# Taking turns between a small and a large expert in a two-layer diffusion backbone

## The chip, the core and the metric

The kernel runs on one core of a Trainium2 chip. The time is the device time of one execution in microseconds (us); the number for a kernel is the median of its runs. The engines are named as the profile names them: PE (TensorE, matrix products), DVE (VectorE), ACT (ScalarE), POOL (GpSimd), SP (SyncE, which issues the weight loads).

## What is computed

The kernel computes a backbone of two layers over 256 latent tokens and 256 context tokens of width 1024. Layer 0 is a gated short convolution and a dense SwiGLU, layer 1 is differential attention and a mixture of experts. The change is in the mixture of experts alone. Cut to that, the reference is:

```python
logits = (a @ w_r) + b_r                       # 256 tokens, 8 experts
top_v, top_i = lax.top_k(logits, 2)            # each token goes to 2 of 8
gates = jax.nn.softmax(top_v, axis=-1)
# every expert e, for the tokens that chose it:
#   y_e = (silu(x_e @ w1[e]) * (x_e @ w3[e])) @ w2[e]     1024 -> 2816 -> 1024
# out[token] = sum over its experts of gate * y_e[token]
h = h + g2 * out
```

All weights are float32, and the result has to be as good as float32. PE's fast form takes operands rounded to a shorter mantissa (fp32r). So most weights are split into a rounded part and the remainder, and both are multiplied.

## The kernel before

**Experts.** Experts 0 and 1 are handled first. The other six are sorted on the chip by how many tokens chose them, and the places 2, 4 and 6 get the three with the fewest tokens (`FEW`, line 37). A place in `FEW` has room for 64 tokens (a "small" expert below), every other place for 128 (a "large" one). Two neighbouring places make a pair: (0,1), (2,3), (4,5), (6,7). The tokens of a pair are gathered together (`gather`, line 1177: eight steps, each of four matmuls into a tile `g` and a few small DVE and ACT operations). `returns` (line 1213) makes the matrices that bring a pair's results back to their tokens.

**Chunks and units.** An expert's weights come in 33 units of 1 MB, three to a chunk, so there are 11 chunks to an expert and 88 in all (`chunks`, line 162: expert by expert). A chunk multiplies two units into a hidden tile (`up`, line 1243; tile `h13`, called h in the profile) and one unit from hidden to output (`down`, line 1282; the accumulators `y`). Between them are the activation (`act`, line 1251) and a turn to the other layout (`hidden`, line 1261). In a large expert a unit costs PE 12 matmuls of 512 columns: the activations too are split in two, and three of the four products are made. In a small expert the two halves of the tokens share one operand, and a unit costs 8.

**The split.** Every unit goes DMA to a raw tile, then ACT rounds it (line 88, tile `wh`), then DVE subtracts (line 92, tile `wl`), each in two halves of 128x1024. There are three pairs of tiles (wh, wl). `Parts.unit` (line 98) hands out the next unit, gives back the pair of the unit before, and at once emits ACT's and DVE's work for the unit two further on. Engines execute in program order, so this work stands in the queues of ACT and DVE between the activation work of the chunks.

**Unsplit units.** In a small expert the second unit of every odd chunk (five of 11) is `whole` (lines 171 to 178): it is multiplied as plain float32 from the raw tile, with four matmuls in place of eight. That takes nothing from ACT or DVE and needs no pair of tiles.

**`hidden` of a small chunk** (lines 1263 to 1273) is a zigzag: PE adds the halves with `fold` (tile `ht`), ACT applies silu (`hg`, line 1267), DVE multiplies (`hg`, line 1268), ACT rounds (`hh`, line 1271), DVE subtracts (`hh`, line 1272). For a large chunk PE transposes, ACT rounds (`hh`, line 1278), DVE subtracts (`hl`, line 1279). DVE also makes the product `ga` (line 1258) in `act`.

**The order of a chunk's work** (loop at line 1345): first unit, `down` of the chunk two before, `hidden` of the chunk before, second unit, `act`. When an expert has ended, `weighted` (line 1296) splits its result (ACT `yh`, DVE `yl`), and `spread` (line 1305) adds it to the tokens in four pieces: each four matmuls into a tile `g`, then two DVE operations on `xl` (line 1315). Gather steps stand at the end of the chunks 3 to 10 of a large expert.

**PSUM** has eight banks: two for `g`, two for `y`, two for h, two for `ht` (lines 1321 to 1324).

Of the kernel before, what the change touches and what calls it, by code (L numbers as in the profile page):

```python
# [11 lines left out]
F32 = mybir.dt.float32  # L12
# [4 lines left out]
OP = mybir.AluOpType  # L17
AX = mybir.AxisListType
PSUM = bass.MemoryType.PSUM

P = 128
D = 1024
KT = D // P
# [12 lines left out]

FEW = (2, 4, 6)
H = P // 2
LAM = 0.8 - 0.6 * math.exp(-0.3)
# [103 lines left out]
def backbone(ctx: ExitStack, tc: tile.TileContext, i, out):  # L143
# [35 lines left out]
    uses += [(NE - 1, 3 * c + 2) for c in (NCH - 2, NCH - 1)]  # L179
    units += [moe_unit(*u) for u in uses]  # L180
# [996 lines left out]
    def gather(pr=None):  # L1177
# [4 lines left out]
        if pr is not None and 2 * pr in FEW:  # L1182
            both = xs[0][0]
            xs[0] = [both[:, :, :H], both[:, :, H:], both]
            cols[0] = slice(H, P)
# [118 lines left out]

    def spread(n, w, back):

        for k in range(4 * n, 4 * n + 4, 2):
            ps = psg.tile([P, 2, T], F32, name="g")
            for j in range(2):
                c = slice((k + j) % 4 * P, ((k + j) % 4 + 1) * P)  # L1310
                for b in range(2):
                    PE.matmul(ps[:, j], w[b][:, c], back, start=b == 0, stop=b == 1)
            for j in range(2):
                x = X[0][k + j]
                V.scalar_tensor_tensor(x, ps[:, j], mod1[20 + k // 2][:, j, 0:1], x, op0=OP.mult, op1=OP.add)  # L1315
# [10 lines left out]
    def acc():  # L1326
        return [psy.tile([P, T2], F32, name=f"y{n}") for n in range(2)]

# [4 lines left out]
    parts.holding = True  # L1333
    res, parted, acts, hids, y = None, deque(), {}, {}, None

    def finish(g):

        result = y
        e, c = chunks[g]
        if c == 0:  # L1340
            result = acc()
        down(result, hids.pop(g), parts.unit(), c == 0, c == NCH - 1)
        return result

    for g, (e, c) in enumerate(chunks):
        n, pr, few_now = e % 2, e // 2, e in FEW
        ps = psh.tile([P, T2], F32, name="h13")
# [6 lines left out]
        if g == 0:  # L1354
            next(run)
            for _ in range(2):
                parts.give(1)
            parts.holding = False
        if g > 1:
            y = finish(g - 2)  # L1360
            if chunks[g - 2][1] == NCH - 1:
                e0 = chunks[g - 2][0]
                res = y, rets[e0 // 2][1][:, e0 % 2:e0 % 2 + 1], rets[e0 // 2][0][:, e0 % 2]
        if g > 0:
            hids[g - 1] = hidden(acts.pop(g - 1), chunks[g - 1][0] in FEW)
        if res is not None:
            parted.extend((m, v, res[2]) for m, v in enumerate(weighted(*res[:2])))
            res = None
        elif parted:
            spread(*parted.popleft())  # L1370
        if g == 1:
# [7 lines left out]
        for k in range(0, 4, 2):  # L1379
            up(ps, got[pr][n], 1, w, [k, k + 1])  # L1380
        acts[g] = act(ps, few_now)
        if parted and c > 1:
            spread(*parted.popleft())
        if n == 0 and c == 4:
            rets[pr] = returns(pr)
        if n == 1 and e < NE - 1:
            if c == 1:
                for t in range(2):
                    onehot(t, pr + 1)
                run = gather(pr + 1)  # L1390
            if 3 <= c < 3 + KT:
                got[pr + 1] = next(run)
    y = finish(g - 1)
    hids[g] = hidden(acts.pop(g))
    y = finish(g)
    for n, w in enumerate(weighted(y, rets[3][1][:, 1:2])):
        spread(n, w, rets[3][0][:, 1])
        write(n)

# [3 lines left out]
    with tc.If(count[0] > 0):  # L1403
        for e in range(NE):
            with tc.If(count[1 + e] > 0):
# [6 lines left out]
                back, gs = returns(e // 2)  # L1412
                y = acc()
                for c in range(NCH):
# [12 lines left out]
                for m, w in enumerate(weighted(y, gs[:, n:n + 1])):  # L1427
                    spread(m, w, back[:, n])
        for n in range(2):
# [82 lines left out]
```

## Time and profile before

| | |
|---|---|
| median of 3 runs | 1592.47 us (1592.3 to 1595.17) |
| the profiled execution's own time | 1594.94 us |
| its span, first to last instruction | 1592.3 us |
| PE busy over the span | 1540.4 us (97%) |
| DVE busy | 1278.5 us (80%) |
| ACT busy | 864.8 us (54%) |
| DMA | 400.35 MB, mean 251 GB/s |
| mixture of experts | from about 820 us to the end |
| mean granted TensorE clock | 0.985 |

In the profile, busy time is the time in which an engine executes. Matmuls overlap in a pipeline, so the time of one matmul in a row is longer than the step from one to the next; the steps are read from the start times. A line of the timeline gives start, length, engine, line of the source, operation, output and inputs, and how many like operations are merged in it. In square brackets stands the time in which the engine was idle just before, and who ended that.

### The profile page before, as it was taken

What the parts mean: (1) busy time and instruction counts of PE and PEld (TensorE: products, weight loads), DVE (VectorE), ACT (ScalarE), POOL (GpSimd) and SP (SyncE); (2) the same over time, 40 slices, a digit from 0 to 9 for tenths busy, and PEclk for the clock granted to TensorE, in tenths of its full rate; (3) what the DMA queues carried; (4) which work ended last, traced back from release to release, by engine and by line L of the source; (5) the groups of instructions that cost most, each with busy time, mean ns of one, the idle gap of its engine ahead of it and who ended that gap; (6) DMA issues with size and microseconds to landing.
All of it is one profiled execution on the core that took longest, in us unless ns stands there. A gap on an engine that the chain in (4) does not pass through costs nothing. (4 is left out here: it accounts for less than half of the span.)

```text
span 1592.3 us, 20866 instructions
## 1 busy us (share of the span) xinstructions
PE 1540.4 (97%) x7569; PEld 1259.1 (79%) x7569; DVE 1278.5 (80%) x1880; ACT 864.8 (54%) x1244; POOL 44.7 (3%) x162
## 2 busy tenths in 40 slices
PE   8899899999999999999889999999999999999997
PEld 7687689888888888888777888877787777877785
DVE  5888887758838848666669899988999889998996
ACT  3232235222212334444557777877788786777774
POOL 0000000000000001211200000000000000000000
PEclk9899999999999999999989999999999999999999
DMA  9345543535527621422338999999999999999990
GB/s 369 111 159 185 191 159 112 184 128 196 204 103 281 251 102 54 159 80 80 133 134 340 362 353 342 342 394 407 364 353 361 388 421 346 347 369 402 395 366 29
DMA packets 55729, 400.35 MB, mean 251 GB/s; under 512 B 6449, under 2 KB 6481, under 8 KB 7105
## 3 DMA queue, kind: packets, MB, share of 16 engines
q1 hardware_dynamic: 55298, 398.50, 66.1%
q8 instruction: 61, 1.00, 0.3%
q0 software_dynamic: 320, 0.44, 0.2%
q14 instruction: 50, 0.41, 0.1%
HBM read 397.87 MB, written 1.05 MB: 251 GB/s over the span
## 5 line engine op out<-in xcount | busy, mean ns | idle before, releaser
L92 DVE TENSOR_TENSOR wl<-rw,wh 128x1024 fp32r<-128x1024 f32 (+1 forms) x208 | 315.9, 1548 | 86.4 <-ACT wh L88 85.8
L88 ACT CAST wh<-rw 128x1024 fp32r<-128x1024 f32 (+1 forms) x207 | 263.3, 1309 | 61.1 <-PE mm L200 56.4
L199 PE MATMUL mm<-ah,wh 128*128 128x512 f32 (+1 forms) x576 | 222.0, 385 | 5.6 <-ACT ah L339 4.7
L201 PE MATMUL mm<-ah,wl 128*128 128x512 f32 (+1 forms) x576 | 221.4, 384 | 5.1 <-DVE wl L92 5.0
L200 PE MATMUL mm<-al,wh 128*128 128x512 f32 (+1 forms) x576 | 221.1, 384 | 0.0
L92 DVE TENSOR_TENSOR wl<-rp,wh 128x1024 fp32r<-128x1024 f32 (+1 forms) x152 | 183.3, 1246 | 17.9 <-ACT wh L88 17.2
L279 DVE SCALAR_TENSOR_TENSOR junk<-ra,cb 128x1024 bf16<-128x1024 f32 x136 | 166.3, 1222 | 3.3
L88 ACT CAST wh<-rp 128x1024 fp32r<-128x1024 f32 (+1 forms) x152 | 155.4, 1070 | 2.6 <-PE h L1240 2.4
L1239 PE MATMUL h<-wh,xs 128*128 128x512 f32 x352 | 142.4, 404 | 0.0
L1241 PE MATMUL h<-wl,xs 128*128 128x512 f32 x352 | 138.9, 395 | 0.0
L1240 PE MATMUL h<-wh,xs 128*128 128x512 f32 x352 | 138.8, 394 | 0.0
L199 PEld LDWEIGHTS mm<-ah,wh 128*128 128x128 f32 x576 | 110.8, 192 | 27.9 <-ACT ah L339 6.0
L201 PEld LDWEIGHTS mm<-ah,wl 128*128 128x128 f32 x576 | 110.3, 192 | 27.7 <-DVE wl L92 7.1
L200 PEld LDWEIGHTS mm<-al,wh 128*128 128x128 f32 x576 | 110.5, 192 | 21.5 <-DVE al L334 0.9
L92 DVE TENSOR_TENSOR wl<-rq,wh 128x1024 fp32r<-128x1024 f32 x102 | 119.5, 1219 | 9.9 <-ACT wh L88 9.4
L92 DVE TENSOR_TENSOR wl<-ra,wh 128x1024 fp32r<-128x1024 f32 x96 | 113.0, 1218 | 6.7 <-ACT wh L88 6.1
L88 ACT CAST wh<-rq 128x1024 fp32r<-128x1024 f32 x102 | 101.2, 1048 | 2.1 <-PE h L1240 2.1
L88 ACT CAST wh<-ra 128x1024 fp32r<-128x1024 f32 x96 | 95.9, 1048 | 0.0
L1241 PE MATMUL y<-wl,hh 128*128 128x512 f32 x220 | 87.4, 397 | 0.6 <-DVE wl L92 0.5
L1239 PE MATMUL y<-wh,hh 128*128 128x512 f32 x220 | 87.1, 396 | 0.5 <-ACT hh L1278 0.5
L1240 PE MATMUL y<-wh,hl 128*128 128x512 f32 x220 | 86.9, 395 | 0.0
L199 PE MATMUL mm<-wh,ah 128*128 128x256 f32 (+1 forms) x256 | 83.7, 327 | 0.0
(330 smaller groups left out, 2988.7 us busy)
## 6 DMA issues: line engine op xcount, KB each, us to landing
rw<-moe SPq DMA_DIRECT2D x81, 1024.0 KB, 7.1
rp<-moe SPq DMA_DIRECT2D x79, 1024.0 KB, 7.1
rw<-w SPq DMA_DIRECT2D x61, 1024.0 KB, 4.8
ra<-moe SPq DMA_DIRECT2D x52, 1024.0 KB, 7.1
rq<-moe SPq DMA_DIRECT2D x52, 1024.0 KB, 7.0
ra<-ada SPq DMA_DIRECT2D x44, 1024.0 KB, 4.9
rx<-ada SPq DMA_DIRECT2D x4, 1024.0 KB, 19.9
rp<-w SPq DMA_DIRECT2D x4, 1024.0 KB, 6.3
```

The costliest lines, as they stand in the source:

```text
L88: self.nc.scalar.copy(hi[:, c0], raw[:, c0])
L92: engine.tensor_tensor(out=lo[:, c], in0=raw[:, c], in1=hi[:, c].bitcast(F32), op=OP.subtract)
L199: PE.matmul(ps, wh, xh, start=first, stop=False)
L200: PE.matmul(ps, wh, xl, start=False, stop=False)
L201: PE.matmul(ps, wl, xh, start=False, stop=last)
L279: V.scalar_tensor_tensor(junk, raw[:, a * D:(a + 1) * D], 1.0, cb[:, s], op0=OP.mult, op1=OP.mult, accum_out=m[:, a, s:s + 1])
L1239: PE.matmul(ps, xh, wh, start=first, stop=False)
L1240: PE.matmul(ps, xl, wh, start=False, stop=False)
L1241: PE.matmul(ps, xh, wl, start=False, stop=last)
```

## The change

Chunks of experts 0 and 1 stay as they are, one expert after the other. From place 2 on, the chunks of the two experts of a pair take turns: small chunk 0, large chunk 0, small chunk 1, and so on. The load order (`uses`) follows from it. Only the chunks 3 and 7 of a small expert have an unsplit unit, so two in place of five, and nine units in all are newly split. Two experts are open at once, so `y` takes four banks; `g` and `ht` fall from two banks to one each. `spread` now does one piece at a time, and a list (`todo`, taken from by `point` three times in a chunk) sets where the pieces and the second result of a pair stand. `returns` stands at chunk 6, and the gather of the next pair runs along both experts' chunks 7 to 10 of the present pair. At the end the last small expert's four pieces stand after the last `down`, ahead of the last large expert's. The small experts' gathered activations get two buffers.

```diff
+WHOLE = (3, 7)
-    chosen, chunks = [], [(e, c) for e in range(NE) for c in range(NCH)]
+    chosen, chunks = [], [(e, c) for e in range(2) for c in range(NCH)]
+    chunks += [(2 * pr + n, c) for pr in range(1, NE // 2) for c in range(NCH) for n in range(2)]
...
-        if e in FEW and c % 2:
+        if e in FEW and c in WHOLE:
             whole.append(len(units) + len(uses))
...
-    psg = fin.enter_context(tc.tile_pool(name="psg", bufs=2, space=PSUM, reuse_waits="tile"))
+    psg = fin.enter_context(tc.tile_pool(name="psg", bufs=1, space=PSUM, reuse_waits="tile"))
...
-    pst = fin.enter_context(tc.tile_pool(name="pst", bufs=2, space=PSUM, reuse_waits="tile"))
+    pst = fin.enter_context(tc.tile_pool(name="pst", bufs=1, space=PSUM, reuse_waits="tile"))
+    def acc(e):
+        return [psy.tile([P, T2], F32, name=f"y{e % 2}{n}") for n in range(2)]
...
+        if g > 1 and chunks[g - 2][1] == NCH - 1:
+            e0 = chunks[g - 2][0]
+            if e0 < 2:
+                result(e0)
+                todo.extend([None, piece, None, piece, piece, None, piece])
...
+                result(e0)
+                todo.extend([None, piece, None, piece, piece, other, None, None, piece, piece, piece, None, piece])
...
-        if n == 0 and c == 4:
+        if n == 0 and c == 6:
             rets[pr] = returns(pr)
...
+        if pr < NE // 2 - 1 and (n == 1 and c >= 1 if pr == 0 else 2 * c + n >= 13):
...
+    finish(g - 1)
     hids[g] = hidden(acts.pop(g))
+    result(NE - 2)
+    finish(g)
+    for m in range(2):
+        for k in range(2):
+            spread(*parted.popleft())
+    result(NE - 1)
+    for m in range(2):
+        for k in range(2):
+            spread(*parted.popleft())
+        write(m)
```

How this moves the order on DVE is seen in the middle of a pair. Before, in the small expert of the pair (4,5) by itself, two chunks hold five splits (`wl`, each row the two halves of a unit), and each chunk the two steps of the zigzag (`hg`, `hh`):

```order
L1272 TENSOR_TENSOR hh<-hg,hh 128x2x64
L92 TENSOR_TENSOR wl_77<-rw_71,wh_76 128x1024 x2
L92 TENSOR_TENSOR wl_79<-rw_73,wh_78 128x1024 x2
L92 TENSOR_TENSOR wl_75<-ra_69,wh_74 128x1024 x2
L1268 TENSOR_TENSOR hg<-ht,hg 128x128
L1272 TENSOR_TENSOR hh<-hg,hh 128x2x64
L92 TENSOR_TENSOR wl_77<-rp_4397,wh_76 128x1024 x2
L92 TENSOR_TENSOR wl_79<-rw_72,wh_78 128x1024 x2
L1268 TENSOR_TENSOR hg<-ht,hg 128x128
L1272 TENSOR_TENSOR hh<-hg,hh 128x2x64
```

Now, in the middle of a pair, on the same engine (`ga` and `hl` belong to the large chunk):

```order
L1272 TENSOR_TENSOR hg<-ht,hg 128x128
L1276 TENSOR_TENSOR hh<-hg,hh 128x2x64
L94 TENSOR_TENSOR wl_77<-rw_71,wh_76 128x1024 x2
L1262 TENSOR_TENSOR ga<-h_11440,ga 128x256
L94 TENSOR_TENSOR wl_79<-rp_4396,wh_78 128x1024 x2
L94 TENSOR_TENSOR wl_75<-rq_6528,wh_74 128x1024 x2
L1283 TENSOR_TENSOR hl<-ht,hh 128x256
L94 TENSOR_TENSOR wl_77<-ra_70,wh_76 128x1024 x2
L94 TENSOR_TENSOR wl_79<-rw_72,wh_78 128x1024 x2
L94 TENSOR_TENSOR wl_75<-rp_4397,wh_74 128x1024 x2
L1272 TENSOR_TENSOR hg<-ht,hg 128x128
L1276 TENSOR_TENSOR hh<-hg,hh 128x2x64
```

A zigzag is now followed by six splits and the two steps of a large chunk before the next zigzag comes; the zigzag itself, and the split that stands right behind it, are as they were.

At the end of the program DVE before had the last expert's `yl` and four pieces (`xl`, two operations each):

```order
L1258 TENSOR_TENSOR ga<-h_12204,ga 128x256
L1279 TENSOR_TENSOR hl<-ht,hh 128x256
L1302 SCALAR_TENSOR_TENSOR yl_12296<-y_11703,gs,yh_12294 128x512
L1302 SCALAR_TENSOR_TENSOR yl_12297<-y_11704,gs,yh_12295 128x512
L1315 SCALAR_TENSOR_TENSOR xl<-g,mod_20_3728,xl 128x256 x2
L1315 SCALAR_TENSOR_TENSOR xl<-g,mod_21_3771,xl 128x256 x2
L1315 SCALAR_TENSOR_TENSOR xl<-g,mod_22_3802,xl 128x256 x2
L1315 SCALAR_TENSOR_TENSOR xl<-g,mod_23_3844,xl 128x256 x2
```

Now the same place has the results of two experts, one behind the other, each piece through the one bank of `g`:

```order
L1262 TENSOR_TENSOR ga<-h_12240,ga 128x256
L1283 TENSOR_TENSOR hl<-ht,hh 128x256
L1306 SCALAR_TENSOR_TENSOR yl_12320<-y_11132,gs,yh_12318 128x512
L1306 SCALAR_TENSOR_TENSOR yl_12321<-y_11133,gs,yh_12319 128x512
L1318 SCALAR_TENSOR_TENSOR xl<-g,mod_20_3728,xl 128x256 x2
L1318 SCALAR_TENSOR_TENSOR xl<-g,mod_21_3771,xl 128x256 x2
L1318 SCALAR_TENSOR_TENSOR xl<-g,mod_22_3802,xl 128x256 x2
L1318 SCALAR_TENSOR_TENSOR xl<-g,mod_23_3844,xl 128x256 x2
L1306 SCALAR_TENSOR_TENSOR yl_12368<-y_11202,gs,yh_12366 128x512
L1306 SCALAR_TENSOR_TENSOR yl_12369<-y_11203,gs,yh_12367 128x512
L1318 SCALAR_TENSOR_TENSOR xl<-g,mod_20_3728,xl 128x256 x2
L1318 SCALAR_TENSOR_TENSOR xl<-g,mod_21_3771,xl 128x256 x2
```

Four pieces and one `yl` pair of the last small expert, which stood among the last large expert's chunks, now stand behind all chunks.

## Rows read from the trace of the kernel before

**Rows 1.** Busy time by stage: length, each engine's busy time, clock, DMA share, GB/s.

```profile
1021.86:1107.77 85.91, 85.86 (x394) 65.13 (x393) 75.85 (x94) 66.70 (x94) 0.00 (x0) 1.00 0.99 390
1107.77:1207.22 99.45, 98.04 (x456) 79.63 (x455) 92.23 (x119) 76.99 (x109) 0.00 (x0) 1.00 0.94 360
1021.86:1207.22 185.36, 183.90 (x848) 144.76 (x847) 168.08 (x212) 143.68 (x202) 0.00 (x0) 1.00 0.96 374
1392.58:1573.64 181.06, 180.37 (x819) 141.50 (x818) 164.87 (x193) 138.78 (x185) 0.00 (x0) 1.00 0.85 338
```

**Rows 2.** DVE timeline in small expert 2: two chunks, five splits.

```profile
1069.54 0.28 DVE L1268 TENSOR_TENSOR hg<-ht,hg 128x128 f32<-128x128 f32 x1
1070.18 0.29 DVE L1272 TENSOR_TENSOR hh<-hg,hh 128x128 fp32r<-128x128 f32 x1 [0.36 <-ACT hh L1271]
1071.13 4.74 DVE L92 TENSOR_TENSOR wl<-ra,wh 128x1024 fp32r<-128x1024 f32 x4 [0.65 <-ACT wh L88]
1075.79 0.28 DVE L1268 TENSOR_TENSOR hg<-ht,hg 128x128 f32<-128x128 f32 x1
...
1077.40 2.36 DVE L92 TENSOR_TENSOR wl<-rw,wh 128x1024 fp32r<-128x1024 f32 x2 [0.67 <-ACT wh L88]
...
1084.31 0.28 DVE L1268 TENSOR_TENSOR hg<-ht,hg 128x128 f32<-128x128 f32 x1
```

**Rows 3.** ACT timeline in the same chunk.

```profile
1084.63 0.30 ACT L1271 CAST hh<-hg 128x128 fp32r<-128x128 f32 x1 [1.88 <-DVE hg L1268]
```

**Rows 4.** PE timeline in the same expert: an unsplit unit's chunk, then a split one.

```profile
1081.60 3.65 PE L1235 MATMUL h<-rp,xl 128*128 128x512 f32 x8
...
1089.63 0.71 PE L1235 MATMUL h<-wh,xl 128*128 128x512 f32 x2
...
1096.15 1.08 PE L1235 MATMUL h<-ra,xl 128*128 128x512 f32 x2
```

**Rows 5.** DVE timeline in large expert 3.

```profile
1122.96 1.40 DVE L1302 SCALAR_TENSOR_TENSOR yl<-y,gs,yh 128x512 fp32r<-128x512 f32 x2
1124.28 2.35 DVE L92 TENSOR_TENSOR wl<-ra,wh 128x1024 fp32r<-128x1024 f32 x2
1126.55 0.42 DVE L1258 TENSOR_TENSOR ga<-h,ga 128x256 f32<-128x256 f32 x1
...
1132.54 1.65 DVE L1315 SCALAR_TENSOR_TENSOR xl<-g,mod,xl 128x256 f32<-128x256 f32 x4
```

**Rows 6.** DVE timeline in expert 3: the splits behind two gather steps.

```profile
1147.75 2.36 DVE L92 TENSOR_TENSOR wl<-rw,wh 128x1024 fp32r<-128x1024 f32 x2 [1.46 <-ACT wh L88]
...
1173.39 2.36 DVE L92 TENSOR_TENSOR wl<-rp,wh 128x1024 fp32r<-128x1024 f32 x2 [0.45 <-ACT wh L88]
```

**Rows 7.** PE timeline in large expert 7: the transposes of two neighbouring chunks.

```profile
1561.85 0.38 PE L1275 MATMUL ht<-ident,ga 128*128 128x128 f32 x2
...
1570.43 0.38 PE L1275 MATMUL ht<-ident,ga 128*128 128x128 f32 x2
```

**Rows 8.** ACT timeline: the copy between the two `g` tiles of `returns`.

```profile
1063.42 0.59 ACT L1220 CAST back<-g 128x512 fp32r<-128x512 f32 x1
```

**Rows 9.** The first gather on PE and DVE; last the busy time of the stage behind.

```profile
820.85 0.41 PE L1196 MATMUL g<-oh,nh 128*128 128x256 f32 x1
821.34 0.53 DVE L1203 TENSOR_SCALAR gx<-g,mod 128x256 f32<-128x256 f32 x1
821.92 0.58 PE L1196 MATMUL g<-oh,nh 128*128 128x256 f32 x1
830.00:842.00 12.00, 10.21 (x39) 7.56 (x38) 8.94 (x15) 9.25 (x13) 0.00 (x0) 0.86 0.48 184
```

**Rows 10.** The end of the program on PE and DVE.

```profile
1579.97 0.40 PE L1241 MATMUL y<-wl,hh 128*128 128x512 f32 x1
1581.89 3.42 DVE L1315 SCALAR_TENSOR_TENSOR xl<-g,mod,xl 128x256 f32<-128x256 f32 x8
1582.91 0.36 PE L1312 MATMUL g<-back,yh 128*128 128x256 f32 x1 [0.59 <-DVE xl L1315]
```

More of the change, by code (lines that the diff above doesn't have):

```diff
@@ L1182, in gather @@
         if pr is not None and 2 * pr in FEW:
-            both = xs[0][0]
+            both = xs[0][pr % 2]
             xs[0] = [both[:, :, :H], both[:, :, H:], both]
@@ L1303, in weighted, with spread @@
         return list(zip(yh, yl))
[L1305 to L1315, printed above, removed]
+    def spread(k, w, back):
+        ps = psg.tile([P, 2, T], F32, name="g")
+        for j in range(2):
+            c = slice((k + j) % 4 * P, ((k + j) % 4 + 1) * P)
+            for b in range(2):
+                PE.matmul(ps[:, j], w[b][:, c], back, start=b == 0, stop=b == 1)
+        for j in range(2):
+            x = X[0][k + j]
+            V.scalar_tensor_tensor(x, ps[:, j], mod1[20 + k // 2][:, j, 0:1], x, op0=OP.mult, op1=OP.add)
     def write(n):
@@ L1333, in backbone, with result, piece, point @@
     parts.holding = True
-    res, parted, acts, hids, y = None, deque(), {}, {}, None
+    parted, acts, hids, ys = deque(), {}, {}, {}
     def finish(g):
-        result = y
         e, c = chunks[g]
         if c == 0:
-            result = acc()
-        down(result, hids.pop(g), parts.unit(), c == 0, c == NCH - 1)
-        return result
+            ys[e] = acc(e)
+        down(ys[e], hids.pop(g), parts.unit(), c == 0, c == NCH - 1)
+    def result(e):
+        back, gs = rets[e // 2]
+        n = e % 2
+        for m, v in enumerate(weighted(ys.pop(e), gs[:, n:n + 1])):
+            parted.extend((4 * m + k, v, back[:, n]) for k in (0, 2))
+    def piece():
+        spread(*parted.popleft())
+    todo = deque()
+    def point():
+        f = todo.popleft() if todo else None
+        if f is not None:
+            f()
     for g, (e, c) in enumerate(chunks):
-        n, pr, few_now = e % 2, e // 2, e in FEW
+        n, pr = e % 2, e // 2
         ps = psh.tile([P, T2], F32, name="h13")
@@ L1358, in backbone, with other @@
             parts.holding = False
+        point()
         if g > 1:
[L1360 to L1363, printed above, removed]
+            finish(g - 2)
         if g > 0:
             hids[g - 1] = hidden(acts.pop(g - 1), chunks[g - 1][0] in FEW)
[L1366 to L1370, printed above, removed]
+        point()
+        if g > 1 and chunks[g - 2][1] == NCH - 1:
[3 more added lines that the diff above has]
+                todo.extend([None, piece, None, piece, piece, None, piece])
+            elif e0 in FEW:
+                def other(e0=e0):
+                    piece()
+                    result(e0 + 1)
+                result(e0)
+                todo.extend([None, piece, None, piece, piece, other, None, None, piece, piece, piece, None, piece])
         if g == 1:
@@ L1380, in backbone @@
             up(ps, got[pr][n], 1, w, [k, k + 1])
-        acts[g] = act(ps, few_now)
-        if parted and c > 1:
-            spread(*parted.popleft())
-        if n == 0 and c == 4:
+        acts[g] = act(ps, e in FEW)
+        point()
+        if n == 0 and c == 6:
             rets[pr] = returns(pr)
-        if n == 1 and e < NE - 1:
-            if c == 1:
+        if pr < NE // 2 - 1 and (n == 1 and c >= 1 if pr == 0 else 2 * c + n >= 13):
+            if pr + 1 not in got:
+                got[pr + 1] = None
                 for t in range(2):
@@ L1412, in backbone @@
                 back, gs = returns(e // 2)
-                y = acc()
+                y = acc(0)
                 for c in range(NCH):
```

17 lines of the change are left out of this document (6 added, 11 removed).

## The prediction

> **What bounds the kernel now.** I read the busy time by stage first, over the third to the last pair of experts, since the change touches little before them. One pair takes 185.36 us, the last one, which gathers for nobody, 181.06 us up to its last chunk's activation [rows 1]. PE is busy for 183.90 of the 185.36 us at the full granted clock, ACT for 143.68, and DVE for 168.08, which is 91% [rows 1]. So PE looks like the bound and DVE like an engine with 17.3 us to spare. The DMA share is 0.96 at 374 GB/s, and it reached 390 GB/s in the small expert's stage [rows 1].
>
> The second look is at DVE's spare time, in its timeline. In a small expert, two chunks with five splits take 1084.31 - 1069.54 = 14.77 us [rows 2]. Three splits take 1084.31 - 1077.40 = 6.91 us, so one takes 2.30. The zigzag takes from 1069.54 to 1071.13, and again from 1075.79 to 1077.40: 1.6 us, of which only 0.57 is work. In the rest DVE waits 0.36 us for ACT's hh and 0.65 us for ACT's next wh. ACT in its turn had waited 1.88 us for DVE's hg [rows 3]. The two engines stand in each other's way: ACT cannot round the next unit before hh, since hh is ahead of it in its queue, and hh needs hg, which DVE reaches late. So DVE's chain is 5 x 2.30 + 2 x 1.6 = 14.7 us, which is all of the 14.77. PE needs for the same two chunks 1096.15 - 1081.60 = 14.55 us [rows 4]. In this stage DVE is a little slower than PE, with 88% busy (75.85 of 85.91).
>
> In a large expert a chunk costs PE 1570.43 - 1561.85 = 8.58 us [rows 7], and DVE three splits with ga and hl at 0.42 each [rows 5], 7.7 us. With gather steps DVE waits again, 1.46 us behind an even step and 0.45 behind an odd one [rows 6]. Adding up a pair for DVE: 61 splits x 2.30 = 140.3; eleven zigzags and eleven times ga and hl, 11 x 2.44 = 26.8; two results, each 1.32 for yl (1124.28 - 1122.96) and four pieces at 0.8 (1.65 for two) [rows 5], 9.0. That is 176.1 us. What is left of 185.4 is 9.3 us, and eight gather steps with 4 x (1.46 + 0.45) = 7.6 us of waits and their own work fill it. So the 17.3 us are not spare: 11 x 1.02 = 11.2 us lie in the zigzags and most of the rest behind the gather steps. **PE and DVE's chain are both full over a pair.**
>
> **The change part by part.** First the turn-taking with three more splits to a pair. In a plain pair of chunks (small split, large) PE needs 6.52 (1096.15 - 1089.63, a split chunk's work [rows 4]) + 8.58 = 15.1 us. DVE's chain needs 6 x 2.30 + 1.6 + 0.84 = 16.2 us. Taking turns does not shorten the zigzag: its two waits come from the order on ACT and DVE, which the new order keeps. So a plain pair runs at DVE's 16.2, and PE begins to wait. Per pair of experts DVE gets 3 x 2.30 = 6.9 us more, and PE is freed of 3 x 1.51 us (8.03 for the chunk with the unsplit unit, 1089.63 - 1081.60, less 6.52 [rows 4]), which is worth nothing while DVE is late. **Three pairs: 20.7 us.** Bounds: below, PE sets the pace (the first rival); above, add the pairs with an unsplit unit. There PE needs 16.6 and DVE 13.9 us, and DVE can use the 2.7 us only as far ahead as the three tile pairs let it. That is two units of PE, 1.9 + 2.8 us (8.58/3 and 8 of a large unit's 12 matmuls), less the half rounding and half subtraction (some 1.0 and 1.2) that must be over: 2.4 us. I take 1 us in all for what is lost there; nothing absorbed would be 6 x 2.7 = 16 us.
>
> The last small expert's yl and pieces leave the pairs: 1.32 + 4 x 0.8 = **-4.5 us** on DVE there.
>
> One bank for g in `returns`: the second tile now waits until ACT has copied the first. The copy is 0.59 us [rows 8], and it stands behind the activation in ACT's queue; PE's small matmuls and DVE's copy of gs follow it. Bounds are 0 and about twice the copy; I take 0.6 each, four times: **2.4 us**.
>
> One bank for g in the first gather, before any chunk: five steps run on PE one after the other. Before, the third waited for the first step's evacuation: it starts at 821.92, and DVE's gx had run from 821.34 to 821.87 [rows 9]. Now each step waits for its own evacuation. The second would start at 821.92 in place of 820.85, and a step then costs its matmuls (0.9, a little under the 1.07 us from the second step's start to the third's, which hold a short wait), 0.53 us of evacuation and two handovers, some 1.55 in place of about 1.0. Five steps make 2.8 us; two more gathers behind the first matmuls have the same pause. The splits of the first chunk stand behind the gather's casts on ACT, so they come later too. **3.5 us**, bounds 2 and 6.
>
> Pieces of expert 0 stand right ahead of two gather steps of expert 1, and share the one bank: PE must wait for DVE's two xl, which stand behind a split and ga. At most 1.3 us twice; DVE's chain is close to PE's there, which hides some. **1.5 us**, bounds 0 and 3.
>
> The end: before, PE's last down ends at about 1580.2, and DVE's last xl at 1581.89 + 3.42 = 1585.31 [rows 10], 5.1 us. Two banks let eight xl run without a pause, and PE's third piece waits 0.59 us. With one bank a piece is PE's four matmuls with their latency (0.63), DVE's two xl (0.86) and two handovers, 1.65 us. Eight pieces and yl between them make some 13.9 us. Against that, the last down but one is a small expert's, 0.9 us shorter, and DVE has no split left at that point. **7 us**, bounds 5 and 9.
>
> DMA: a pair now asks for the same 66 units in more time, at steadier demand, so it stays hidden. The loads wait for tiles on SP; nothing is moved past it. Experts 0 and 1 keep their chunks.
>
> **How the sum stands.** 20.7 + 1 - 4.5 + 2.4 + 3.5 + 1.5 + 7 = 31.6 us on the profiled execution's 1594.94 us: 1626.5 us. That execution lies 2.5 us above the median of 1592.47, so I forecast 1624 us, 2.0% slower.
>
> **Rivals.** First, PE sets the pace and the change gives what PE saves. PE's work in a pair is 183.9 us [rows 1]; less 3 x 1.51 it is 179.4. DVE's bare work is 168.08 + 6.9 = 175.0. If the waits in DVE's chain fell from 17.3 us to under 4.4 us, PE would be the bound, and a pair would take 6.0 us less: -18 for three, some -2 for the four pieces that leave a pair, and +14.4 for `returns`, start, early pieces and end. That is 1589.3, or **1587 us** by the median. For it speaks that DVE runs without a pause from 1122.96 to 1126.55 in a large expert [rows 5]; against it, that each zigzag has the same 1.02 us of waits, whether DVE was late or not, and that nothing in its queue was moved between hg, hh and the next split. The Trainium skill says for kernels whose most-contended engine changes over time that interleaving these regimes may improve performance (Perfetto Trace Analysis, Optimization Strategy), and that occupancy is a fair measure for VectorE (the same page, Identifying the Most-Contended Engine). By that rule this rival's time would come out; I set rows 2 and 3 against it, where an engine that is 88% busy is the slower one.
>
> Second, PE's waits cost it its clock. In the stage from 830 to 842 PE was busy for 10.21 of 12 us and the granted clock was 0.86, a mean of its levels of 1.2 and 2.4 GHz [rows 9]; the time lost by that is (1 - 0.86) x 12 = 1.7 us. With some 1 us of wait in each of 33 pairs of chunks, one pair in three losing as much gives 19 us more, **1643 us**. Against it: over expert 3, where PE was busy for 98.04 of 99.45 us, the clock stayed at 1.00 [rows 1], and PE would still be busy for over nine tenths.
>
> Third, DVE's splits lag only where gather steps or pieces add to them, and the plain pairs run at 15.1 us because the two units of lead carry them. Then 1.1 us x about 15 plain pairs is not lost, and the time is about **1608 us**: slower still.
>
> **How the numbers follow.** 0.68 for the forecast, 0.12 for the first rival, 0.08 for the second, 0.12 for the third. The forecast's own range is 1612 to 1636, from the bounds of the start, the end and the unsplit pairs. With the third rival and half of the second the range is 1600 to 1643; it leaves out the first rival and part of the second. About 0.2% (3.2 us) is what a measurement of this kernel can tell from no change. Faster by more: 0.12; within: 0.04; slower: 0.84.
>
> **What would show it.** In the profile after, DVE's timeline within a pair of chunks without an unsplit unit should repeat every 16.2 us, with the waits of 0.36 and 0.65 us in the zigzag and none elsewhere, and PE should show waits for wl (line 94). A pair of experts should take 190 to 194 us, with DVE busy for 175 of them, and PE for some 179. The first five gather steps should be 1.5 us apart, and the eight pieces at the end 1.65. The prediction is wrong if pairs of chunks repeat at 15.1 us, or if the two waits of the zigzag are gone from DVE.

## The result, and the profile after

The changed kernel takes 1638.66 us (median of 4 runs, 1635.46 to 1643.01), the kernel before 1593.82 us beside it. The ratio on record is 1.0292, 95% interval 1.0279 to 1.0306; the two medians lie 44.8 us apart. The forecast was 1624 us, with a range of 1600 to 1643. The time lies in the range, near its upper end; the forecast itself was 15 us too low.

The page of the changed kernel, span and busy times:

```profile
span 1633.4 us, 20833 instructions
PE 1545.9 (95%) x7569; PEld 1257.8 (77%) x7569; DVE 1296.9 (79%) x1898; ACT 878.9 (54%) x1262; POOL 46.8 (3%) x162
```

DVE has 18 us more work than before (nine more splits at the 2.30 us of the prediction would be 20.7), and PE is busy for a smaller share of a longer span. Neither says where 45 us went. The busy time by stretch does (length, busy time of PE, PEld, DVE, ACT, POOL, granted clock, DMA share, GB/s). Each stretch ends at an activation on ACT: the first one, that of expert 1's first chunk, of its last, then of the last chunk of each pair; the last row is the tail. After:

```profile
815.40:835.64 20.24, 15.65 (x58) 12.00 (x58) 8.88 (x25) 9.75 (x22) 0.00 (x0) 0.68 0.01 1
835.64:932.43 96.79, 94.00 (x419) 75.37 (x420) 87.62 (x110) 72.23 (x92) 0.00 (x0) 1.00 0.91 345
932.43:1030.73 98.30, 93.81 (x429) 76.47 (x428) 86.29 (x115) 71.44 (x102) 0.00 (x0) 0.98 0.84 323
1030.73:1221.53 190.80, 184.94 (x844) 144.79 (x842) 168.88 (x203) 145.89 (x203) 0.00 (x0) 0.99 0.96 363
1221.53:1417.20 195.67, 185.81 (x846) 144.10 (x846) 174.25 (x218) 148.06 (x209) 0.00 (x0) 0.99 0.93 356
1417.20:1602.95 185.75, 178.47 (x810) 140.05 (x811) 169.02 (x198) 143.93 (x192) 0.00 (x0) 0.99 0.85 327
1602.95:1633.40 30.45, 13.85 (x50) 9.78 (x48) 12.03 (x24) 3.29 (x7) 0.00 (x0) 0.67 0.10 37
```

The same stretches before, where [rows 1] do not have them:

```profile
819.86:834.27 14.41, 13.28 (x58) 10.93 (x58) 8.87 (x25) 9.58 (x23) 0.00 (x0) 0.80 0.01 2
834.27:930.61 96.34, 95.15 (x419) 76.59 (x420) 87.62 (x110) 72.24 (x91) 0.00 (x0) 0.98 0.92 349
930.61:1021.86 91.25, 91.25 (x426) 74.71 (x425) 84.49 (x110) 70.32 (x99) 0.00 (x0) 1.00 0.91 341
1573.64:1592.30 18.66, 9.16 (x42) 6.49 (x40) 6.45 (x13) 2.13 (x4) 0.00 (x0) 0.86 0.17 61
```

The differences, beside the terms of the forecast:

| stretch | before | after | difference | forecast |
|---|---|---|---|---|
| first gather to the first activation | 14.4 | 20.2 | +5.8 | 3.5 |
| on to expert 1's first chunk | 96.3 | 96.8 | +0.5 | 0.6 (one `returns`) |
| expert 1 | 91.3 | 98.3 | +7.0 | 1.5 |
| three pairs | 551.8 | 572.2 | +20.4 | 19.0 (20.7 + 1 - 4.5 + 3 x 0.6) |
| tail | 18.7 | 30.5 | +11.8 | 7 |
| sum | 772.4 | 818.0 | +45.6 | 31.6 |

(The part ahead of the first gather, which the change leaves alone, was 4.5 us shorter in this execution, 815.40 for 819.86, so the spans differ by 41.) Each column comes from one execution, and the four of the changed kernel lie 7.55 us apart (1635.46 to 1643.01 us, mean granted clock 0.978 to 0.973), so a difference of a few us in one stretch can be the clock's.

**The plain pair of chunks** on DVE, between two zigzags, answers to [rows 2]:

```profile
1306.97 0.28 DVE L1272 TENSOR_TENSOR hg<-ht,hg 128x128 f32<-128x128 f32 x1
1307.62 0.29 DVE L1276 TENSOR_TENSOR hh<-hg,hh 128x128 fp32r<-128x128 f32 x1 [0.37 <-ACT hh L1275]
1308.57 2.36 DVE L94 TENSOR_TENSOR wl<-rw,wh 128x1024 fp32r<-128x1024 f32 x2 [0.66 <-ACT wh L90]
1310.85 0.42 DVE L1262 TENSOR_TENSOR ga<-h,ga 128x256 f32<-128x256 f32 x1
1311.18 2.35 DVE L94 TENSOR_TENSOR wl<-rp,wh 128x1024 fp32r<-128x1024 f32 x2
1313.45 2.35 DVE L94 TENSOR_TENSOR wl<-rq,wh 128x1024 fp32r<-128x1024 f32 x2
...
1320.60 2.35 DVE L94 TENSOR_TENSOR wl<-rw,wh 128x1024 fp32r<-128x1024 f32 x2
1322.87 0.28 DVE L1272 TENSOR_TENSOR hg<-ht,hg 128x128 f32<-128x128 f32 x1
```

The pair repeats after 1322.87 - 1306.97 = 15.90 us, and the only waits in it are the two of the zigzag, 0.37 and 0.66 us. Over the three pairs of experts DVE has another wait, of which the trace before lists none (total in us, times, longest):

```profile
DVE hg L1272 <- ACT hg L1271: 13.8, 10, 2.0
```

It stands behind each of the six unsplit units (0.61 to 1.86 us, 8.0 in all) and behind each of the three `returns` (1.64 to 2.00 us, 5.5 in all): ACT's hg waits for PE's `fold` there, so in these places DVE waits for PE.

**Expert 1.** In this first pair the gather for the next pair does not run along the chunks 7 to 10: it starts one chunk earlier than before, at chunk 2 of expert 1 in place of 3, beside the pieces of expert 0. PE and DVE where a piece stands right ahead of a gather step:

```profile
950.25 0.28 PE L1315 MATMUL g<-back,yl 128*128 128x256 f32 x1
953.31 0.38 PE L1200 MATMUL g<-oh,nh 128*128 128x256 f32 x1 [2.78 <-DVE xl L1318]
...
966.88 0.39 PE L1200 MATMUL g<-oh,nh 128*128 128x256 f32 x1 [1.72 <-DVE xl L1318]
```

```profile
949.79 2.34 DVE L94 TENSOR_TENSOR wl<-rq,wh 128x1024 fp32r<-128x1024 f32 x2
952.06 0.41 DVE L1262 TENSOR_TENSOR ga<-h,ga 128x256 f32<-128x256 f32 x1
952.40 0.86 DVE L1318 SCALAR_TENSOR_TENSOR xl<-g,mod,xl 128x256 f32<-128x256 f32 x2
954.09 0.54 DVE L1207 TENSOR_SCALAR gx<-g,mod 128x256 f32<-128x256 f32 x1 [0.84 <-PE g L1200]
956.09 2.36 DVE L94 TENSOR_TENSOR wl<-rw,wh 128x1024 fp32r<-128x1024 f32 x2 [1.46 <-ACT wh L90]
```

The piece is done on PE at 950.5, but DVE reads it only behind a split and `ga`. PE waits 2.78 us for the one bank; DVE then waits 0.84 us for the gather step that it made late, and 1.46 us for ACT's next rounding, which stands behind that step's casts. So one full bank stops three engines in turn. The same happens once more one chunk later, with 1.72 us.

**The end** on PE, first matmuls of the last piece of expert 6 and of the pieces of expert 7, answers to [rows 10]:

```profile
1615.54 0.39 PE L1315 MATMUL g<-back,yh 128*128 128x256 f32 x1 [0.97 <-DVE xl L1318]
...
1617.34 0.55 PE L1315 MATMUL g<-back,yh 128*128 128x256 f32 x1 [1.06 <-DVE xl L1318]
...
1619.88 0.58 PE L1315 MATMUL g<-back,yh 128*128 128x256 f32 x1 [0.97 <-DVE xl L1318]
...
1622.16 0.55 PE L1315 MATMUL g<-back,yh 128*128 128x256 f32 x1 [1.06 <-DVE xl L1318]
...
1624.33 0.58 PE L1315 MATMUL g<-back,yh 128*128 128x256 f32 x1 [0.97 <-DVE xl L1318]
```

and the last row of DVE:

```profile
1625.59 0.88 DVE L1318 SCALAR_TENSOR_TENSOR xl<-g,mod,xl 128x256 f32<-128x256 f32 x2 [1.32 <-PE g L1315]
```

Every piece waits for the evacuation of the one before. Those of expert 6 are 1.7 us apart, those of expert 7 2.2 to 2.5. In this execution the last `down`, ahead of the pieces, was slow too, at the lower granted clock:

```profile
1606.20:1609.70 3.50, 3.50 (x10) 2.71 (x10) 1.41 (x2) 0.70 (x2) 0.00 (x0) 0.54 0.00 0
```

From its first matmul to its last it took 4.44 us; in each of the other kernels of this study, those with one bank among them, 2.88 or 2.89. So 1.6 us of this tail are the clock of this one execution.

### The profile page after: what moved, and what is told of

The parts are those of the page before. It is cut to its first block, busy times and chain, and to the rows that moved or that the text cites. A ratio compares the mean times of both kernels' runs of the same rounds, so it can differ in the third digit from the quotient of the medians.

```text
span 1633.4 us, 20833 instructions
## 1 busy us (share of the span) xinstructions
PE 1545.9 (95%) x7569; PEld 1257.8 (77%) x7569; DVE 1296.9 (79%) x1898; ACT 878.9 (54%) x1262; POOL 46.8 (3%) x162
## 4 chain that ended last, share of the span: by engine, by line
## 5 line engine op out<-in xcount | busy, mean ns | idle before, releaser
L94 DVE TENSOR_TENSOR wl<-rw,wh 128x1024 fp32r<-128x1024 f32 (+1 forms) x220 | 330.0, 1529 | 81.4 <-ACT wh L90 80.6
L90 ACT CAST wh<-rw 128x1024 fp32r<-128x1024 f32 (+1 forms) x219 | 275.4, 1295 | 62.2 <-PE mm L204 56.4
L1243 PE MATMUL h<-wh,xs 128*128 128x512 f32 x352 | 146.1, 415 | 0.0
L1244 PE MATMUL h<-wh,xs 128*128 128x512 f32 x352 | 140.6, 400 | 0.0
L94 DVE TENSOR_TENSOR wl<-ra,wh 128x1024 fp32r<-128x1024 f32 x100 | 117.8, 1218 | 9.7 <-ACT wh L90 8.7
L90 ACT CAST wh<-ra 128x1024 fp32r<-128x1024 f32 x100 | 100.0, 1049 | 0.9 <-PE h L1244 0.9
```

The source lines that it names most:

```text
L90: self.nc.scalar.copy(hi[:, c0], raw[:, c0])
L94: engine.tensor_tensor(out=lo[:, c], in0=raw[:, c], in1=hi[:, c].bitcast(F32), op=OP.subtract)
L1243: PE.matmul(ps, xh, wh, start=first, stop=False)
L1244: PE.matmul(ps, xl, wh, start=False, stop=False)
```

## The experiments

Theory: DVE's chain, with the zigzag's waits in it, sets the pace in the pairs (20 us), and the one bank of `g` costs the rest (25 us). The main rival is that PE or the bank sets the pace in the pairs too. The ratios are to the kernel before, 1592 us beside these runs; stretches as in the table above.

| kernel | us | ratio (95%) | start | expert 1 | pairs | tail |
|---|---|---|---|---|---|---|
| changed kernel | 1638.7 | 1.0292 (1.0279 to 1.0306) | 20.2 | 98.3 | 572.2 | 30.5 |
| five | 1635.0 | 1.0267 (1.0250 to 1.0284) | 20.2 | 98.2 | 569.2 | 29.2 |
| b_two | 1612.2 | 1.0126 (1.0109 to 1.0142) | 14.3 | 91.3 | 573.0 | 18.9 |
| zig | 1616.7 | 1.0162 (1.0143 to 1.0180) | 20.2 | 98.3 | 552.1 | 30.0 |
| b_zig | 1587.7 | 0.9968 (0.9957 to 0.9980) | 14.4 | 91.3 | 549.1 | 18.7 |
| bank | 1617.9 | 1.0163 (1.0146 to 1.0180) | 14.7 | 92.3 | 573.8 | 22.2 |
| b_g1 | 1650.8 | 1.0364 (1.0347 to 1.0381) | 22.0 | 97.0 | 593.3 | 22.4 |
| zig_bank | 1591.7 | 0.9998 (0.9989 to 1.0008) | 13.5 | 92.4 | 546.3 | 23.2 |
| b_zig3 | 1586.6 | 0.9964 (0.9951 to 0.9976) | 13.5 | 91.3 | 548.0 | 18.6 |
| b_zig_two | 1588.4 | 0.9986 (0.9977 to 0.9996) | 14.6 | 91.3 | 549.4 | 18.9 |
| zig_bank_tail | 1591.5 | 1.0000 (0.9990 to 1.0009) | 14.5 | 92.3 | 550.6 | 19.2 |
| zig_bank_tail_one | 1588.3 | 0.9981 (0.9971 to 0.9990) | 14.5 | 92.3 | 547.8 | 19.3 |

### Undoing one part, and doing one part alone: the unsplit units

Five unsplit units in the changed kernel (`five`), and two in the kernel before (`b_two`):

```diff
-WHOLE = (3, 7)
+WHOLE = (1, 3, 5, 7, 9)
```

> The changed kernel with five unsplit units to a small expert again (the second unit of chunks 1, 3, 5, 7 and 9), still taking turns. If DVE's chain of splits sets the pace of the pairs of experts, nine units fewer to split take up to 9 x 2.3 = 20.7 us off it, less what PE's longer chunks (16.6 us to a pair of chunks) give back: some 15 us faster than the changed kernel, about 1623 us. If the single bank of g or PE itself sets the pace, PE has 9 x 1.5 = 13.6 us more work: 1640 to 1652 us.

```diff
-        if e in FEW and c % 2:
+        if e in FEW and c in (3, 7):
```

> The kernel before, expert by expert and with its two banks, with only the chunks 3 and 7 of a small expert unsplit: the one other part of the change by itself. If DVE's chain is full, nine more splits of 2.3 us make it about 20 us slower than before, 1614 us, with the small experts' chunks at 8.5 us where both units are split and the large ones as they were. If PE is the bound, it saves 13.6 us: 1580 us. If the taking of turns is what costs, this one stays near 1594.

In the kernel before, two instead of five cost 573.0 - 551.8 = 21.2 us in the pairs, all of the loss of `b_two`: a newly split unit costs 21.2/9 = 2.36 us, one split of DVE. In the changed kernel, giving the three back gains only 3.0 us in the pairs, which one or two falls of the clock would make as well. `b_two` came within 2 us of the theory's number; my expectation for `five` was wrong. What it overlooked is that a unit given back to PE costs PE 1.51 us, and with turns taken PE has no room for it. In `five`, in a pair whose small chunk has an unsplit unit, DVE no longer leads but waits for PE (through ACT):

```profile
1324.71 0.29 DVE L1272 TENSOR_TENSOR hg<-ht,hg 128x128 f32<-128x128 f32 x1 [1.86 <-ACT hg L1271]
```

The changed kernel has the same wait behind its own two unsplit units, as said above. A split and an unsplit pair together cost PE 15.1 + 16.6 = 31.7 us, which is 15.85 each, and two split ones cost DVE 15.9 each. So the two halves of the change are not additive: either alone costs 17 to 21 us in the pairs (569.2 and 573.0 for 551.8), both together 20.4.

### The zigzag

The second half of a small chunk's `hidden` (ACT's hh, DVE's subtraction) is put behind the emission of the next unit's rounding and splitting, in the changed kernel (`zig`) and in the kernel before (`b_zig`). Nothing is added or removed (`halves` holds the removed lines):

```diff
-            hb = px.tile([P, T], F32R, name="hh").rearrange("p (f b s) -> p f b s", f=2, b=2)
...
-            return [hb]
+            return g
...
         w = parts.unit()
+        if g > 0 and chunks[g - 1][0] in FEW:
+            hids[g - 1] = halves(hids[g - 1])
```

> The changed kernel with the second half of a small chunk's zigzag (ACT's hh and DVE's subtraction) put behind the next unit's rounding and split in program order, so that ACT no longer waits for DVE's hg with a unit's rounding behind it. No operation is added or left out. If the zigzag's 1.02 us of waits on DVE are part of the pace, the three pairs of experts lose up to 33 x 1.02 = 34 us, down to PE's floor of some 180 us a pair: about 27 us faster than the changed kernel, 1612 us. If PE's waits for the single bank or its clock set the pace, it stays at 1639.

> The kernel before with the zigzag cut in the same way. PE is busy for 183.9 of 185.4 us of a pair there, so at most 1.5 us a pair can be had: 1590 to 1593 us if PE and DVE's chain are both full; much less than that, 1570, if DVE's chain alone were the bound.

In `zig` (1616.7 us; 1612 expected) the pairs fall from 572.2 to 552.1 us, and a plain pair of chunks from 15.9 to 15.07. DVE and, last, the busy time of one plain pair:

```profile
1298.30 0.29 DVE L1279 TENSOR_TENSOR hg<-ht,hg 128x128 f32<-128x128 f32 x1
1298.74 2.36 DVE L94 TENSOR_TENSOR wl<-rw,wh 128x1024 fp32r<-128x1024 f32 x2 [0.15 <-ACT wh L90]
1301.02 0.29 DVE L1269 TENSOR_TENSOR hh<-hg,hh 128x128 fp32r<-128x128 f32 x1
```

```profile
1300.34:1315.41 15.07, 15.07 (x71) 12.37 (x70) 14.87 (x17) 12.96 (x18) 0.00 (x0) 1.00 1.01 425
```

The two waits of 1.03 us have become one of 0.15, since a split now stands between hg and hh, and ACT can round the next unit while DVE makes hg. PE is busy all of the time, DVE for 14.87 of 15.07: both are full, and PE sets the pace, at the 15.1 us that the prediction had worked out for it. (The DMA share is 1.01 in this pair, but in the three pairs of this trace no engine waits for a load.) Start, expert 1 and tail stay late, so these are another cost. In the kernel before the same reorder gives only 2.7 us in the pairs: there, with five unsplit units, PE is right behind DVE (1587.7 us; I had expected 1590 to 1593).

The same with other numbers of unsplit units in the kernel before:

```diff
-        if e in FEW and c % 2:
+        if e in FEW and c in (3, 7):
```

> The kernel before with the reorder of the zigzag and the change's two unsplit units in a small expert. Theory (three more splits cost 20 us in the kernel before only because DVE waits in the zigzag; without those waits a small expert costs DVE 77.6 us and PE 74.7, beside 79.3 of PE with five unsplit): 1585 to 1590, that is, nothing is lost against the reorder alone. Rival (a newly split unit costs DVE's 2.3 us whatever the order): 1587.7 + 20 = 1608.

```diff
-        if e in FEW and c % 2:
+        if e in FEW and c in (1, 5, 9):
```

> The kernel before with the reorder of the zigzag and three unsplit units in a small expert (chunks 1, 5 and 9) instead of five. By the chains: a small expert's 11 chunks cost DVE 11 x 7.47 less 2.30 for each unsplit unit, and PE 11 x 6.52 plus 1.51 for each; with three that is 75.3 and 76.2 us, with five 70.7 and 79.3, where PE is now the bound. Theory (PE sets the pace once the zigzag's waits are gone, so that fewer unsplit units pay): 2 to 3 us less for each of three small experts than the reorder alone, 1578 to 1582 us. Rival (the lead of two units is too short, DVE is late again in the chunks that are split): 1587 to 1593. Rival (loading is the bound in that stage, its DMA share is 0.99): 1586 to 1589.

`b_zig_two` tells the most: the step that cost 21.2 us in the kernel before costs 0.3 with the reorder (549.4 for 549.1). A pair, in `b_two` and in `b_zig_two`:

```profile
1018.16:1210.33 192.17, 183.72 (x848) 143.00 (x847) 174.96 (x218) 148.99 (x209) 0.00 (x0) 1.00 0.95 361
```

```profile
1017.34:1201.64 184.30, 181.13 (x848) 145.82 (x847) 173.12 (x218) 149.06 (x208) 0.00 (x0) 0.99 0.96 377
```

DVE's work is the same to 1%; only its order differs. At 91% DVE set the pace; at 94% PE is busy for 98% of the pair, and all that it waits for is DVE's hh, 3.0 us. (The Trainium skill calls occupancy a fair measure of the distance to the roofline for VectorE: Perfetto Trace Analysis, Identifying the Most-Contended Engine. Here it did not tell the two cases apart.) `b_zig3` is the fastest kernel of the study, 0.36% below the kernel before, but its gain over `b_zig` is 1 us, not the 6 to 9 expected: between two and five unsplit units the pairs stay within 1.5 us, so the balance of DVE and PE over a small expert no longer decides. The rival that loading sets the pace there had named 1586 to 1589 us, and the time lies in that; but no engine waits for a load in the three pairs of this trace, and PE's only waits in them are for DVE's hh, 8.0 us. What decides was not tried further.

### The bank

`g` and `ht` draw from one pool of two banks, in the changed kernel (`bank`); and one bank for `g` in the kernel before, all else as it was (`b_g1`):

```diff
-    psg = fin.enter_context(tc.tile_pool(name="psg", bufs=1, space=PSUM, reuse_waits="tile"))
-    pst = fin.enter_context(tc.tile_pool(name="pst", bufs=1, space=PSUM, reuse_waits="tile"))
+    psg = fin.enter_context(tc.tile_pool(name="psg", bufs=2, space=PSUM, reuse_waits="tile"))
...
-        pt = pst.tile([P, T], F32, name="ht")
+        pt = psg.tile([P, T], F32, name="g")
```

> The changed kernel with one thing different: the tiles g and ht draw from one pool of two banks instead of one bank each, so that two g tiles in a row, or a g and an ht, do not wait for each other's evacuation. The order of work is untouched. Theory (the one bank of g is what the start, the early pieces and the end cost above the forecast): the five first gather steps go back from 1.74 to about 1.0 us, the stretch of expert 1's chunks from 98.3 to about 92 us, the eight pieces at the end from 1.7 to 2.5 us apart to about 1.1, the returns give 0.9 each: 4.6 + 6 + 4 + 3.6 = about 18 us less than the changed kernel's 1638.7, so 1618 to 1624, while plain pairs of chunks stay at 15.9 us. Rival (those stretches are late because DVE's and ACT's queues have more in them, not for the bank): 1633 to 1639.

```diff
-    psg = fin.enter_context(tc.tile_pool(name="psg", bufs=2, space=PSUM, reuse_waits="tile"))
+    psg = fin.enter_context(tc.tile_pool(name="psg", bufs=1, space=PSUM, reuse_waits="tile"))
```

> The kernel before with one thing different: g has one bank instead of two (ht keeps two, all else and the order as before). Theory (the bank alone carries these costs): +4.6 us at the first gather, +0.6 to 0.9 at each of four returns, +2 to 3 us at the end with its four pieces, and a few us in expert 1, where pieces and gather steps follow each other: 1602 to 1610 us. Rival (the bank costs only where pieces stand right ahead of gather steps, as the changed order puts them, and at the first gather): 1596 to 1600. Nothing at all: 1592.

`bank` takes 5.5 us from the start, 6.0 from expert 1 and 8.3 from the tail, and nothing from the pairs (573.8 for 572.2). So the one bank is the cause of all but 1 us of what expert 1 lost and of some 7 us of the tail's 11.8: 1.6 of the 8.3 are the slow `down` above, and from `zig` to `zig_bank` (below), where neither has it, the tail falls by 6.8. (The edit lets `ht` share the two banks too; `b_g1` changes `g` alone.) In the pairs the sum hides two things. PE's wait for the second tile of `returns`, in the changed kernel and in `bank`:

```profile
1332.62 1.16 PE L1229 MATMUL g<-by,oh 128*128 128x1 f32 x8 [1.97 <-ACT back L1224]
1321.65 1.08 PE L1229 MATMUL g<-by,oh 128*128 128x1 f32 x8 [1.44 <-DVE hl L1283]
```

In two pairs the step with `returns` is 0.5 us shorter in `bank` (18.81 and 18.84 us for 19.33 and 19.37, from activation to activation), near the 0.6 that I charged. In the last pair it is 2.6 us longer (20.39 for 17.78): there the granted clock fell behind this wait in `bank`, and thirteen matmuls start 0.43 us apart in place of 0.23; in the changed kernel it stayed at 1.00. (The Trainium skill asks that independent matmul groups rotate through PSUM banks, so that one's evacuation overlaps the next's matmuls: Perfetto Trace Analysis, Matmuls. The start, expert 1 and the tail agree, with some 18 us; the pairs, where DVE sets most of the pace, gain nothing by it here.) On the end of DVE in `bank`, the first four pieces run without a pause, as before the change:

```profile
1600.97 3.43 DVE L1318 SCALAR_TENSOR_TENSOR xl<-g,mod,xl 128x256 f32<-128x256 f32 x8 [1.81 <-PE g L1315]
1604.32 1.40 DVE L1306 SCALAR_TENSOR_TENSOR yl<-y,gs,yh 128x512 fp32r<-128x512 f32 x2
```

`b_g1` missed every expectation by 40 us or more. Start and expert 1 lose as in the changed kernel, but the pairs lose 41.5 us. The waits of PE in one pair:

```profile
PE g L1312 <- DVE xl L1315: 9.7, 4, 4.6
PE g L1225 <- ACT back L1220: 1.5, 1, 1.5
```

The order before puts two pieces directly behind each other. With one bank, the second waits until DVE has come to the first, up to 4.6 us, four times in a pair. By these traces, it is `spread` of one piece at a time, with chunk work between, that makes the one bank bearable in the changed kernel's pairs. Where users of `g` still follow each other directly, at the start, in expert 1 and at the end, the bank shows.

### Both together, and the end

Both edits on the changed kernel (`zig_bank`):

> The changed kernel with both edits: the second half of a small chunk's hidden steps stands behind the next unit's rounding and splitting, and g and ht share two banks. If the two costs are apart (DVE's zigzag in the plain pairs, the bank at the start, the early pieces and the end), the gains add: 22 us from the one and 18 from the other, so 1597 to 1603 us, still above the kernel before, since the last small expert's result stays behind the last chunk. If the bank's wait and the zigzag hide each other, 1606 or more.

It is better than expected: 1591.7 us, no different from the kernel before, with pairs of 546.3 us, 5.4 less than before the change. In `zig_bank` PE sets the pace, and now the bank in `returns` counts: the step with `returns` is 16.82 us in each pair, for 17.80 and 17.81 in `zig` (from activation to activation) and 19.37 in the last pair of `zig`, where the clock fell behind it. What is lost against that is the tail, 23.2 us.

In the last pair, the small expert three chunks ahead, so that its pieces stand among the large one's chunks (`zig_bank_tail`), then with one unsplit unit (`zig_bank_tail_one`):

```diff
     chunks += [(2 * pr + n, c) for pr in range(1, NE // 2) for c in range(NCH) for n in range(2)]
+    last = chunks[-2 * NCH:]
+    chunks[-2 * NCH:] = sorted(last, key=lambda k: (k[1] + 3 * (k[0] % 2), k[0] % 2))
...
-    result(NE - 2)
     finish(g)
-    for m in range(2):
-        for k in range(2):
-            spread(*parted.popleft())
     result(NE - 1)
```

> Both edits on the changed kernel (reorder, shared banks), and in the last pair the small expert runs three chunks ahead, so that its result is added to the tokens among the large expert's last chunks and only the last large expert's four pieces are left at the end. Theory (the tail's 4.5 us above the kernel before are the last small expert's result behind the last chunk): the tail falls from 23.2 to about 18.7 us and the last pair gains 0 to 2: 1587 to 1590. Rival (what stands at the end moves into the pair and costs as much there): 1591 to 1593.

```diff
-WHOLE = (3, 7)
+WHOLE = (5,)
```

> The same kernel with one unsplit unit in a small expert (chunk 5) instead of two. A plain pair of chunks costs PE 15.07 us with the reorder, and DVE 6 x 2.30 + 0.57 + 0.84 = 15.2, so both are full; one unsplit unit less saves PE 1.5 us in a pair of experts and gives DVE 2.3 more. Theory (PE sets the pace, DVE has slack beside the unsplit unit and gather steps): 1.5 us less for each of three pairs, 4 us below the kernel with two. Rival (DVE is as full as PE): 0 to 3 us above it.

The tail falls by 4.0 us as planned, and the last pair takes 184.06 us in place of 179.81, 4.3 more. The time is the rival's, but the trace does not show its cause. The last three large chunks, which now have the moved pieces among them, take 26.3 us, and three plain ones of the kernel before take 25.8. Most of the loss lies at the head of the pair, where three small chunks now follow one another beside the results of the pair before. PE's longest wait there:

```profile
1417.00 1.09 PE L1298 MATMUL y<-wh,hh 128*128 128x512 f32 x2 [2.56 <-DVE hh L1271]
```

and the eight matmuls from there on are 0.43 us apart, at the lower clock, which is 1.6 us more. So it is not shown that the moved work had to be paid in the pair. One unsplit unit in place of two gives 3.2 us, near the 4 expected; by the traces the pairs give 2.8 of it, 0.6 in each of the first two (1.5 expected) and 1.5 in the last, where the clock hardly falls this time. The turn-taking can be had for nothing with both edits, but in none of these runs is it worth more than the reorder alone in the old order of chunks (1586.6 to 1588.4).

## Why the prediction was right, and where its sizes were off

- **DVE's chain sets the pace in the pairs: right.** Plain pairs repeat at 15.90 us (16.2 said), with the two waits named and no other; pairs of experts take 190.8 and 195.7 (190 to 194; the second lies above), DVE is busy for 174.25 in the second (175). PE's busy time is 185.8 there, not 179: a matmul is recorded as 0.39 us long where they start 0.23 apart, so short pauses count as busy (the same matmuls in `zig_bank` show 180.5 in 185.9 us). `zig` and `b_zig_two` show the cause: without the waits in the zigzag the three pairs lose nothing. The first rival (PE sets the pace) asked for just this; its condition is not met by the change, but by moving one step in two queues. The third rival (15.1 us by the lead of two units) falls with the 15.90.
- **Three more splits to a pair, 20.7 us: the right total by one of two ways.** `b_two` shows it alone, `five` shows that with turns taken nearly the same 17.4 us is lost without them, to PE. The step "worth nothing while DVE is late" was right for the changed kernel, and the prediction did not need the other; my sum for turn-taking alone would leave the pairs where they were, and they lose 17.4 us. What they lose it to is seen in part: a pair of chunks with gather steps takes 18.4 us where a plain one takes 15.9, 2.5 us more, whereas before a large chunk with one step took 9.1 for 8.6 (from activation to activation). That these steps lost the slack that DVE had in the large expert fits this, but no run isolates it.
- **The unsplit pairs (1 us said) and `returns` (0.6 each said): both too small, and the sum of the pairs owes something to luck.** DVE waits 8.0 us for PE behind the six unsplit units, where I had let its lead take up nearly all, and 5.5 us behind the three `returns`, where PE waits 1.96 to 1.98 us for the bank, more than my bound of twice the copy. Together these waits are 13.5 us where 2.8 were charged. Yet the pairs lost 20.4 us, near the 19.0 forecast, so something gave about as much back. I had called DVE's chain full over a pair before the change, with 2.30 us for a split and 0.42 for `ga` and for `hl`; its steps start 2.27, 0.33 and 0.34 us apart, which is also why a plain pair takes 15.90 us and not 16.2. By these steps the chain had 61 x 0.03 + 11 x 0.17 = 3.7 us more room in a pair than I counted, 11 us in three: an estimate, and no run isolates it. The three pairs differ too (5.4, 10.3 and 4.7 us more than before), and none isolates the -4.5 us for the result that leaves.
- **Early pieces, 1.5 us said, 7.0 measured: the term that was mis-sized most.** I took PE's wait for the bank as at most 1.3 us, twice, and let DVE hide some. The waits are 2.78 and 1.72 us, and behind the first follow DVE's 0.84 and 1.46 us and a slower clock (below), since the late gather step is itself a link of the chain PE, DVE, ACT, DVE. `bank` gives 6.0 of it back.
- **The start, 3.5 us said, 5.8 measured,** within the bounds of 2 and 6. The five steps came every 1.9 us (815.40, then 817.47 to 823.09 for the other four), not 1.5, and the granted clock over the stretch fell from 0.80 to 0.68. `bank` brings the whole of it back but 0.3.
- **The end, 7 us said, 11.8 measured,** above the bound of 9. Of this 1.6 us are the slow last `down`. Pieces of expert 6 are 1.7 us apart, as said; those of expert 7 are 2.2 to 2.5 apart, and the granted clock fell to the lower level among them (below). From the last activation to DVE's last xl it is 23.5 us for 11.7.
- **The second rival, the clock, has a part of it,** though a small one in the pairs, where I had put it: there the granted clock is 0.99 over a pair. Its falls stand behind waits of PE, most of them for the one bank: in the start, in expert 1, among the last pieces, and in two of the three pairs behind `returns`, where the step takes 19.33 and 19.37 us and 17.78 in the pair in which the clock stayed.

## What to carry to other kernels

Before an engine's idle time is counted as room, look at which of its waits come from the order of its own queue and its neighbour's: an idle microsecond between two steps that two engines hand to and fro is not room until something else is put between them, and doing that was worth 20 us here. When a buffer is halved, charge every place where two users of it follow each other directly, with the reader's whole queue in between (here a split and `ga`), and what that reader feeds next. An undo tells what a part costs in the changed kernel, and doing the part alone what it costs in the old one; only the two together show whether the costs add.

## What the runs showed of the hardware that was not expected

Behind a wait of PE of 2 to 3 us the clock fell for a while in some places and not in others. The granted clock in expert 1 of the changed kernel, around the wait of 2.78 us, and then at the end, among the pieces of expert 6 and of expert 7:

```profile
947.00:953.30 6.30, 3.53 (x19) 2.80 (x17) 6.26 (x9) 2.65 (x4) 0.00 (x0) 1.00 0.91 326
954.70:957.60 2.90, 2.90 (x8) 2.27 (x7) 1.51 (x2) 2.90 (x5) 0.00 (x0) 0.50 0.56 232
957.70:964.00 6.30, 6.30 (x31) 5.20 (x30) 4.98 (x7) 3.32 (x5) 0.00 (x0) 0.98 0.65 190
1610.50:1616.00 5.50, 2.50 (x16) 1.91 (x15) 2.63 (x6) 0.69 (x1) 0.00 (x0) 1.00 0.00 0
1617.40:1625.50 8.10, 5.08 (x16) 3.70 (x16) 3.73 (x8) 0.00 (x0) 0.00 (x0) 0.50 0.23 84
```

While PE waits in expert 1 the clock is still at its 2.4 GHz level; it falls to the 1.2 GHz level when PE is already working again, for some 3 us, and then comes back. At the end it falls after four pieces with waits of about 1 us each between them and stays low. In the first place eight matmuls took 3.38 us (954.63 to 958.01) instead of 1.87, so a wait of 2.78 us cost 1.5 us more than itself. Behind the wait of 1.72 us one chunk later the matmuls keep their 0.23 us. Behind the waits in `returns`, all of 1.96 to 1.98 us, it fell in the first two pairs and not in the third; the second and the third:

```profile
1333.90:1336.60 2.70, 2.70 (x7) 2.12 (x8) 2.70 (x4) 1.00 (x2) 0.00 (x0) 0.50 0.99 410
1529.00:1533.00 4.00, 4.00 (x20) 3.30 (x20) 4.00 (x5) 3.14 (x4) 0.00 (x0) 1.00 1.02 395
```

Behind a wait of 2.85 us for a piece in the second pair (1242.92) the granted clock stayed at 1.00, behind one of 2.84 us in the third (1438.59) it fell to 0.50. So one execution does not tell what such a wait costs: for `returns` it was the wait alone, or the wait and 1.6 us more.

And the second bank of `g`: to be without it costs 58.6 us in the old order (`b_g1`, 1650.8 for 1592.2) and some 21 in the new one (1638.7 for 1617.9 in `bank`, where `ht` shares the two banks). The traces put the difference to the pieces that stand directly behind each other; no run isolates it.
